# Two query tiles per group of sums over v, chunk-wise decayed keys, and side work dealt in half products

## The chip, the cores and the metric

One NeuronCore of a Trainium2 chip runs the whole kernel as one program. The metric is the device time of one execution in microseconds, from runs of the kernel; lower is better. A profile of one execution gives the engines' instructions: TensorE (PE; its weight loads PEld), VectorE (DVE), ScalarE (ACT), GpSimd (POOL) and SyncE (SP, which issues DMAs here).

## What is computed

A transformer layer on 512 tokens of width 1024, all in float32: a SwiGLU feed-forward (width 2816) with residual and layer norm, a token mixer with residual and layer norm, and a second feed-forward. The mixer adds two gated branches of one input projection:

```python
# sliding window attention, blocks of 128 queries, each against its own and the previous block of keys
scores = einsum('bnqkgd,bnskd->bnkgqs', qb, kb) * 64**-0.5      # masked, with a sink per head
p = exp(scores - m); probs = p / (sum(p) + exp(sink - m))
out = einsum('bnkgqs,bnskd->bnqkgd', probs, vb)                 # 16 query heads, 4 kv heads, width 64
# HGRN2 recurrence, 8 heads of 128, chunks of 64 tokens
f = lb + (1 - lb) * sigmoid(f_logit); k = 1 - f; gc = cumsum(log f)      # within a chunk
q_dec = q * exp(gc); k_inv = k * exp(-gc); k_end = k * exp(g_last - gc)
o = causal(q_dec @ k_inv.T) @ v + q_dec @ state;  state = state * exp(g_last) + k_end.T @ v
y = o * rsqrt(mean(o**2) + eps) * norm_g * silu(og)
merged = sigmoid(gate_a) * (y_attn @ w_pa) + sigmoid(gate_h) * (y @ w_ph);  out = merged @ w_out
```

## The kernel before

Large products keep float32 accuracy with operands split into two rounded halves (`split`, L72): ScalarE casts the high half (`whi`), VectorE subtracts to get the low half (`wlo`), and TensorE runs three matmuls for each pair (`mm3`, L104, and `Quads.mul`, L272). Weights stream through SP's queue as 128 x 1024 slabs (`raw`), five buffers; `whi` and `wlo` have four each. A `quad` (L324) computes a 2 x 2 block product with seven products (Strassen's form), for which VectorE also adds weight blocks (`wsum`, L291). A product is 2 x 12 matmuls of 256 columns. Two of the seven products of a quad are left to the next one (`late`, `flush`). `Pipe` (L233) keeps one product prepared ahead of the one that runs.

Attention and the recurrence are side work. They are written as generators, and `Side` (L201) takes steps of them between products: each `tick` adds `rate` to a credit, and each whole unit buys one step, up to the next `yield`. `drain` takes all that is left. The order in which the program is traced gives each instruction its priority; a planner then orders every engine's queue by these priorities and by when it believes operands to be ready, and each engine works its queue off in that order. `tc.issue_after` fixes one instruction behind another on the same engine.

Attention works in four chunks (two pairs of kv heads, each with two query heads of each half) of four query tiles of 128. For each tile `scores` (L716) makes the scores of four heads in two banks and adds mask and sink; `outputs` (L740) exponentiates, normalises (L757), transposes the weights (`transposed`, L110, matmul line L113), copies them out (L763), and sums over v: for each half of the array's columns (`hf`) and each of one or two key blocks one matmul with 64 stationary columns (L770), all in one bank, then one copy (L773) and a store to `ya_dram`. The next tile's scores are traced before the outputs of this one. `both` mixes in the rope of the next chunk's queries, one step after every fourth.

The recurrence (`heads`, L981) runs per head `decays` (L881) and, one head behind, `recur` (L917). Two tiles of keys, `ei` (inverse decay) and `ke` (decay to the chunk's end), lie one after the other. For each block of 128 tokens, one matmul takes all 128 columns of `ei` (L924) and a second one, with 64 stationary columns of `ke`, replaces the scores between the two chunks of the block (L926). A mask copy, the transposed keys (L936), state updates (L942, L951) and outputs (L957, L959) follow; then ScalarE squares, VectorE reduces, GpSimd raises to the power -1/2 (L968), VectorE scales (L970), TensorE transposes (L973), and y goes to `yh_dram`. Rates are 8, 6, 8 and 12 steps per product. After the last products `sums` projects `ya_dram` (its eight products `run` carry the last side work), then `yh_dram`.

Only these functions change; both feed-forwards share `Quads.mul` but have no side work.

Of the kernel before, what the change touches and what calls it, by code (L numbers as in the profile page):

```python
# [20 lines left out]
P = 128  # L21
# [21 lines left out]
def body(ctx, tc, a):  # L43
# [156 lines left out]

    class Side:  # L201

# [8 lines left out]
        def step(self):  # L211
            while self.queue:
                if next(self.queue[0], self) is not self:
                    return True
                self.queue.pop(0)
            return False

        def tick(self):
            if self.queue:
                self.due += self.rate  # L220
            while self.due >= 1.0:
                self.due -= 1.0
                if not self.step():
                    self.due = 0.0

        def drain(self):
            while self.step():
                pass
            self.due = 0.0
# [3 lines left out]
    class Pipe:  # L233
# [9 lines left out]
        def pump(self, depth=0):  # L243
            while len(self.queue) > depth:
                run, ops = self.queue.pop(0)
                run(ops)
                side.tick()
# [14 lines left out]
    class Quads:  # L262
# [8 lines left out]
        def mul(self, bk, w, n, first, last):  # L271
            wh, wl = (t.rearrange("p (k j c) -> p k j c", j=2, c=P) for t in w)  # L272
            xh, xl = self.x.get(n)
            for j in range(2):
                reg = bk[:, j * 256:(j + 1) * 256]

                def mm(w, x, first=False, last=False):
                    nc.tensor.matmul(reg, lhsT=w, rhs=x, start=first, stop=last, skip_group_check=True)  # L278

                for k in range(4):  # L280
                    mm(wh[:, k, j], xh[:, k], first=first and j == 0 and k == 0)
                    mm(wh[:, k, j], xl[:, k])
                for k in range(4):
                    mm(wl[:, k, j], xh[:, k], last=last and k == 3)

# [311 lines left out]
    def tok_major(src, b_bc, dst):  # L597

        parts = []

        def prep(t):
            if not parts:
                parts.extend(slab(src[i]) for i in range(2))
            return t

        def run(t):
            acc = bank("A")
            for k in range(KT):
                c = (k % 4) * 256
                mm3(acc[:, :256], x1.tok(k, t), [w[:, c:c + 256] for w in parts[k // 4]], k == 0, k == KT - 1)  # L610
            nc.vector.tensor_tensor(out=dst[:, t], in0=acc[:, :256], in1=b_bc, op=ALU.add)
        return lambda t: pipe.push(lambda: prep(t), run)
# [127 lines left out]
    def outputs(pp, n, ip, neg, nm, y):  # L740
# [24 lines left out]
        yield  # L765
        o = bank("B")
        for hf in range(2):
            g = 2 * pp + hf
            for kk in range(kb):
                nc.tensor.matmul(o[hf * HD:(hf + 1) * HD, :256],  # L770
                                 lhsT=v_sb[:, n + 1 - kb + kk, g * HD:(g + 1) * HD],
                                 rhs=pts[kk][:, hf * 256:(hf + 1) * 256], start=kk == 0, stop=kk == kb - 1)
        nc.scalar.copy(out=y, in_=o[:, :256].rearrange("p (i c) -> p i c", i=2))  # L773

    def chunk(pp, ip, qs):
        ahead = yield from scores(pp, 0, ip, qs)
        for n in range(TT):
# [3 lines left out]
            y = room(5, [P, 2, P])  # L781
            yield from outputs(pp, n, ip, *now, y)
            h = 4 * pp + 2 * ip
            nc.sync.dma_start(out=ya_dram[h:h + 2, :, n * P:(n + 1) * P].rearrange("i p c -> p i c"), in_=y)
            yield

    def both(work, other, n):

        res = None
        for i, _ in enumerate(work):  # L790
            yield
# [50 lines left out]
    side.rate = 2.0  # L842
# [16 lines left out]
    def par(t, e):  # L859

        return t.rearrange("p (t e s) -> p t e s", e=2, s=CH)[:, :, e]
# [19 lines left out]
    def decays(h):  # L881
# [15 lines left out]
        func(out=ei, in_=gc, func=AF.Exp, scale=-1.0)  # L897
        nc.vector.tensor_tensor(out=ch(ke), in0=ch(gc)[:, :, CH - 1:CH].broadcast_to([P, NC, CH]), in1=ch(gc),
# [8 lines left out]
        nc.vector.tensor_tensor(out=ei, in0=ei, in1=kk, op=ALU.mult)  # L907
        nc.vector.tensor_tensor(out=ke, in0=ke, in1=kk, op=ALU.mult)
# [6 lines left out]
        return q, ei, ke, q2, de, dd  # L915

    def recur(h, q, ei, ke, q2, de, dd):  # L917
# [3 lines left out]
        sp = bank("B")  # L921
        for t in range(TT):
            tsl = slice(t * P, (t + 1) * P)
# [9 lines left out]
        nc.vector.tensor_tensor(out=par(ke, 0)[:, :TT - 1], in0=par(ke, 0)[:, :TT - 1],  # L933
                                in1=de[1][:, :TT - 1].broadcast_to([P, TT - 1, CH]), op=ALU.mult)
        yield
        kp = transposed([ke[:, t * P:(t + 1) * P] for t in range(TT - 1)])  # L936
# [35 lines left out]
        yield  # L972
# [33 lines left out]
    next_heads(0, 8.0)  # L1006
# [3 lines left out]
    next_heads(1, 6.0)  # L1010
# [6 lines left out]
    next_heads(2, 8.0)  # L1017
    quad_to(a["w_fqg"][5], pairs[3].q, pairs[3].g)
    vals(3)
    next_heads(3, 12.0)  # L1020
# [6 lines left out]
    def sums(n, src, wname, slots, combine):  # L1027
# [165 lines left out]
```

## Time and profile before

| | |
|---|---|
| time, median of 3 runs | 1295.9 us (1295.33 to 1296.37) |
| profiled execution | 1297.03 us, span 1294.9 us |
| PE busy | 1253.3 us, 97% |
| DVE busy | 936.2 us, 72% |
| ACT busy | 626.4 us, 48% |
| attention stage, recurrence stage | 454 to 606 us, 620 to 835 us |

The span runs from the first to the last instruction of the profiled execution. Busy is the union of an engine's instructions; TensorE's matmuls are pipelined, so their records overlap, and a start-to-start distance tells more than a duration. A float32 matmul that is not split leaves two records.

### The profile page before, as it was taken

How to read it: one execution, taken by the hardware profiler on the slowest of the kernel's cores; microseconds unless marked ns; L12 is line 12 of the kernel's file. 1: busy time of each engine (PE TensorE's matmuls, PEld its weight loads, DVE VectorE, ACT ScalarE, POOL GpSimd, SP SyncE). 2: the span in 40 equal slices, each digit the busy share in tenths (PEclk: the TensorE clock that was granted, in tenths of full speed). 3: DMA queues.
4: the chain of work that ended last, by engine and by line, in shares of the span. 5: the costliest groups of instructions: out<-in, count | busy, mean ns of one | idle time of the engine just before them, and what ended most of it. 6: DMA issues, size and time to landing. Idle time of an engine off the chain costs nothing.

```text
span 1294.9 us, 21771 instructions
## 1 busy us (share of the span) xinstructions
PE 1253.3 (97%) x9040; PEld 1170.0 (90%) x9040; DVE 936.2 (72%) x1288; ACT 626.4 (48%) x891; POOL 75.9 (6%) x53
## 2 busy tenths in 40 slices
PE   7999999999998999999999999899999999999997
PEld 7999999988898989898998987788899999998886
DVE  7987878623499998997778776464798787784325
ACT  5645555411156667667653746342355445463110
POOL 2000000000031100100011010000120000000001
PEclk9999999999999999999999999999999999999998
DMA  6424233532233443223223243574233423354211
GB/s 239 134 96 131 83 114 131 179 96 88 94 104 105 144 134 99 91 98 101 71 77 102 83 130 122 168 255 131 98 115 115 128 85 115 102 162 143 84 47 65
DMA packets 53315, 150.75 MB, mean 116 GB/s; under 512 B 5856, under 2 KB 15072, under 8 KB 53216
## 3 DMA queue, kind: packets, MB, share of 16 engines
q1 hardware_dynamic: 49184, 135.72, 32.3%
q10 hardware_dynamic: 4032, 13.63, 3.0%
q8 instruction: 71, 1.16, 0.4%
q14 instruction: 28, 0.23, 0.1%
HBM read 134.65 MB, written 14.68 MB: 115 GB/s over the span
## 4 chain that ended last, share of the span: by engine, by line
PE 56%; DVE 7%; issue 2%; POOL 1%; ACT 1%; DMA 1%; DVEq 0%; SPq 0%; POOLq 0%; ACTq 0%
PE A L278 30%; PE A L106 4%; PE A L108 4%; PE A L107 4%; PE B L107 2%; PE B L106 2%; PE B L108 2%; PE B L113 2%; PE B L770 1%; DVE wlo L75 1%; PE B L924 1%; POOL rs L968 1%; DVE wsum L291 1%; PE B L926 1%; PE B L728 1%
## 5 line engine op out<-in xcount | busy, mean ns | idle before, releaser
L278 PE MATMUL A<-x,whi 128*128 128x256 f32 x3840 | 550.8, 285 | 14.4 <-ACT whi L74 7.5
L278 PEld LDWEIGHTS A<-x,whi 128*128 128x128 f32 x3840 | 499.9, 193 | 20.1 <-ACT whi L74 7.8
L75 DVE TENSOR_TENSOR wlo<-raw,whi 128x1024 fp32r<-128x1024 f32 (+1 forms) x186 | 225.5, 1214 | 185.3 <-ACT whi L74 184.0
L74 ACT CAST whi<-raw 128x1024 fp32r<-128x1024 f32 (+1 forms) x186 | 192.9, 1040 | 324.2 <-PE A L108 132.0
L278 PE MATMUL A<-x,wlo 128*128 128x256 f32 x1920 | 313.3, 284 | 1.6 <-DVE wlo L75 1.6
L278 PEld LDWEIGHTS A<-x,wlo 128*128 128x128 f32 x1920 | 267.2, 193 | 2.5 <-DVE wlo L75 2.0
L74 ACT CAST whi<-wsum 128x1024 fp32r<-128x1024 f32 x128 | 134.3, 1050 | 153.9 <-PE A L278 96.0
L75 DVE TENSOR_TENSOR wlo<-wsum,whi 128x1024 fp32r<-128x1024 f32 x128 | 156.2, 1220 | 12.5 <-ACT whi L74 12.2
L107 PE MATMUL A<-wlo,x 128*128 128x256 f32 (+1 forms) x360 | 115.4, 321 | 0.0
L106 PE MATMUL A<-whi,x 128*128 128x256 f32 (+1 forms) x360 | 115.3, 320 | 0.0
L108 PE MATMUL A<-whi,x 128*128 128x256 f32 (+1 forms) x360 | 115.0, 320 | 0.0
L291 DVE TENSOR_TENSOR wsum<-raw 128x1024 f32<-128x1024 f32 x64 | 87.6, 1373 | 2.7 <-POOL x L129 2.0
L291 DVE TENSOR_TENSOR wsum<-raw,wsum 128x1024 f32<-128x1024 f32 x64 | 78.0, 1218 | 0.8
L106 PEld LDWEIGHTS A<-whi,x 128*128 128x128 f32 x360 | 68.5, 190 | 5.1
L108 PEld LDWEIGHTS A<-whi,x 128*128 128x128 f32 x360 | 68.3, 190 | 4.9
L107 PEld LDWEIGHTS A<-wlo,x 128*128 128x128 f32 x360 | 68.4, 190 | 4.6
L107 PE MATMUL B<-wlo,x 128*128 128x512 f32 (+1 forms) x200 | 69.8, 349 | 0.0
L106 PE MATMUL B<-whi,x 128*128 128x512 f32 (+1 forms) x200 | 69.6, 348 | 0.0
L108 PE MATMUL B<-whi,x 128*128 128x512 f32 (+1 forms) x200 | 69.3, 347 | 0.0
L412 POOL TENSOR_TENSOR rstd<-ve,pw 128x1 f32<-128x1 f32 x12 | 16.2, 1352 | 759.9 <-DVE ve L410 758.6
L106 PE MATMUL A<-x,whi 128*128 128x512 f32 (+1 forms) x160 | 59.8, 374 | 0.0
L107 PE MATMUL A<-x,whi 128*128 128x512 f32 (+1 forms) x160 | 59.3, 371 | 0.0
(172 smaller groups left out, 1536.6 us busy)
## 6 DMA issues: line engine op xcount, KB each, us to landing
raw<-in_w_dram SPq DMA_DIRECT2D x130, 512.0 KB, 3.6
raw<-in_w_fqg_dram SPq DMA_DIRECT2D x24, 512.0 KB, 3.7
raw<-in_w_q_dram SPq DMA_DIRECT2D x8, 512.0 KB, 3.7
raw<-in_w_ga_dram SPq DMA_DIRECT2D x8, 512.0 KB, 3.4
raw<-in_w_gh_dram SPq DMA_DIRECT2D x8, 512.0 KB, 3.8
raw<-in_w_i_dram SPq DMA_DIRECT2D x8, 512.0 KB, 3.8
raw<-in_w_pa_dram SPq DMA_DIRECT2D x8, 512.0 KB, 4.4
g<-x_spill ACTq DMA_DIRECT2D x8, 512.0 KB, 4.5
```

The source lines that it names most:

```text
L74: nc.scalar.copy(out=hi, in_=src)
L75: nc.vector.tensor_tensor(out=lo, in0=src, in1=hi, op=ALU.subtract)
L106: nc.tensor.matmul(out, lhsT=lh, rhs=rh, start=first, stop=False, **kw)
L107: nc.tensor.matmul(out, lhsT=lh, rhs=rl, start=False, stop=False, **kw)
L108: nc.tensor.matmul(out, lhsT=ll, rhs=rh, start=False, stop=last, **kw)
L113: nc.tensor.transpose(out=tp[:, j * P:(j + 1) * P], in_=b, identity=ident)
L278: nc.tensor.matmul(reg, lhsT=w, rhs=x, start=first, stop=last, skip_group_check=True)
L291: nc.vector.tensor_tensor(out=t, in0=x, in1=y, op=ALU.add)
L412: nc.gpsimd.tensor_tensor(out=rstd, in0=ve, in1=pw, op=ALU.pow)
L728: nc.tensor.matmul(out, lhsT=qs[i][:, hf, qsl], rhs=k_hi[pp][:, hf, ksl], start=True, stop=False)
L770: nc.tensor.matmul(o[hf * HD:(hf + 1) * HD, :256], lhsT=v_sb[:, n + 1 - kb + kk, g * HD:(g + 1) * HD], rhs=pts[kk][:, hf * 256:(hf + 1) * ...
L924: nc.tensor.matmul(sp[:, tsl], lhsT=ei[:, tsl], rhs=q[:, tsl], start=True, stop=True)
```

## The change

The side work's credit is now given in shares: half a product's rate in the middle of a product and half at its end, in the projections a quarter after every second of eight key blocks. A step may return `PAUSE`, which ends the tick and leaves the rest of the credit for the next one. Pauses stand behind the normalisation of the attention weights, behind their copies, and behind the normalisation of a head's output. The rates become 3 (attention, was 2), 4, 4, 4 and 9.

`outputs` is cut into `probs` and `weigh`. `weigh` sums over v for two query tiles at once: two banks, one for each half of the columns, 6 or 8 matmuls whose halves alternate, the tile that came last first, all others fixed behind the first. The transposed weights of odd tiles are copied into the rooms of that tile's scores. The output is copied in two halves of 64 partitions, and stored once per two tiles.

In the recurrence `ei` and `ke` lie chunk by chunk in one tile (64 columns of `ei`, 64 of `ke`, and so on). The scores of a block are two matmuls with 128 stationary columns each and 64 moving ones: the first chunk's queries against its `ei` and `ke`, the second chunk's against the first's `ke` and its own `ei`.

```diff
+    PAUSE = object()
         def step(self):
             while self.queue:
-                if next(self.queue[0], self) is not self:
-                    return True
+                r = next(self.queue[0], self)
+                if r is not self:
+                    return r or self
                 self.queue.pop(0)
-            return False
+            return None
-        def tick(self):
+        def tick(self, share):
             if self.queue:
-                self.due += self.rate
+                self.due += self.rate * share
             while self.due >= 1.0:
                 self.due -= 1.0
-                if not self.step():
+                r = self.step()
+                if r is PAUSE:
+                    break
+                if r is None:
                     self.due = 0.0
...
-                run(ops)
-                side.tick()
+                side.tick(run(ops) or 0.5)
...  (Quads.mul)
+                if j == 0:
+                    side.tick(0.5)
...  (tok_major)
+                if k == KT // 2:
+                    side.tick(0.5)
...  (probs, from outputs)
-        yield
+        yield PAUSE
+        tps = [transposed([neg[j // 2][:, j % 2, kk * P:(kk + 1) * P] for j in range(4)]) for kk in range(kb)]
         pts = []
         for kk in range(kb):
-            tp = transposed([neg[j // 2][:, j % 2, kk * P:(kk + 1) * P] for j in range(4)])
-            pt = room(6 + kk)
-            nc.scalar.copy(out=pt, in_=tp)
+            pt = neg[kk].rearrange("p i c -> p (i c)") if n % 2 else room(6 + kk)
+            nc.scalar.copy(out=pt, in_=tps[kk])
             pts.append(pt)
+        return pts
+    def weigh(pp, n, pts, y):
+        o = [bank("B") for _ in range(2)]
+        first = None
+        for i in (1, 0):
+            kb = len(pts[i])
+            for m, kk in enumerate(reversed(range(kb))):
+                for hf in range(2):
+                    g = 2 * pp + hf
+                    with tc.issue_after(first) if first else ExitStack():
+                        mm = nc.tensor.matmul(o[hf][hf * HD:(hf + 1) * HD, i * 256:(i + 1) * 256],
+                                              lhsT=v_sb[:, n + i + 1 - kb + kk, g * HD:(g + 1) * HD],
+                                              rhs=pts[i][kk][:, hf * 256:(hf + 1) * 256], start=m == 0, stop=m == kb - 1)
+                    first = first or mm.ins
         for hf in range(2):
...
+            nc.scalar.copy(out=y[h].rearrange("p i n c -> p n i c"),
+                           in_=o[hf][h].rearrange("p (n i c) -> p n i c", n=2, i=2))
...  (chunk)
+            pts.append((yield from probs(pp, n, ip, *now)))
+            yield PAUSE
+            if n % 2:
+                y = room(5, [P, 2, 2, P])
+                weigh(pp, n - 1, pts[-2:], y)
...  (decays)
-        lf, ke = room(2 + h % 2), room(4 + h % 2)
-        e = big(10 if h % 2 == 0 else 4)
-        eg, ei = e[:, 0], e[:, 1]
+        lf, eg = room(2 + h % 2), room(4 + h % 2)
+        ek = big(10 if h % 2 == 0 else 4, [P, NC, 2, CH])
+        ei, ke = ek[:, :, 0], ek[:, :, 1]
...  (recur)
-            nc.tensor.matmul(sp[:, tsl], lhsT=ei[:, tsl], rhs=q[:, tsl], start=True, stop=True)
-            lo, hi = slice(t * P, t * P + CH), slice(t * P + CH, (t + 1) * P)
-            nc.tensor.matmul(sp[:CH, hi], lhsT=ke[:, lo], rhs=q[:, hi], start=True, stop=True)
+            for e in range(2):
+                c = slice(t * P + e * CH, t * P + (e + 1) * CH)
+                k0 = t * 2 * P + e * CH
+                nc.tensor.matmul(sp[:, c], lhsT=rows[:, k0:k0 + P], rhs=q[:, c], start=True, stop=True)
...  (behind the scaling by rs)
-        yield
+        yield PAUSE
         oT = transposed([on[:, t * P:(t + 1) * P] for t in range(TT)])
...  (sums, run)
+                if k and k % 2 == 0:
+                    side.tick(0.25)
...
+            return 0.25
```

## Rows read from the trace of the kernel before

**Rows 1.** The page's busy table: engine, busy us, share of span, instructions.
```profile
PE 1253.3 (97%) x9040; PEld 1170.0 (90%) x9040; DVE 936.2 (72%) x1288; ACT 626.4 (48%) x891; POOL 75.9 (6%) x53
```

**Rows 2.** Stages: window, length, busy PE, PEld, DVE, ACT, POOL, clock, DMA share, GB/s.
```profile
405.00:454.00 49.00, 45.80 (x379) 45.14 (x378) 48.40 (x77) 32.05 (x53) 5.52 (x3) 1.00 0.42 135
454.00:606.00 152.00, 149.96 (x1165) 135.50 (x1163) 138.56 (x337) 106.01 (x242) 8.59 (x5) 0.99 0.34 104
500.00:525.00 25.00, 25.00 (x209) 23.70 (x208) 19.50 (x44) 18.17 (x39) 0.00 (x0) 1.00 0.38 114
540.00:565.00 25.00, 24.66 (x190) 24.00 (x191) 24.47 (x68) 17.43 (x44) 1.30 (x1) 0.93 0.18 59
620.00:835.00 215.00, 203.80 (x1497) 187.58 (x1496) 154.34 (x230) 115.56 (x156) 18.86 (x16) 1.00 0.32 104
```

**Rows 3.** PE's waits in 405:454 and 620:840: total us, times, longest us.
```profile
PE B L113 <- DVE r L757: 2.2, 1, 2.2
...
PE B L113 <- DVE r L970: 9.4, 7, 2.5
```

**Rows 4.** PE timeline, runs of two and four sums: start, length, operation, count.
```profile
496.77 0.65 PE L770 MATMUL B<-r,g 128*64 128x256 f32 x4
...
507.43 0.64 PE L278 MATMUL A<-x,wlo 128*128 128x256 f32 x4
508.00 1.09 PE L770 MATMUL B<-r,g 128*64 128x256 f32 x8
...
509.24 0.28 PE L729 MATMUL B<-g,g 128*128 128x256 f32 x1
```

**Rows 5.** PE timeline, a cut run and one out of step.
```profile
477.81 0.48 PE L278 MATMUL A<-x,whi 128*128 128x256 f32 x2
478.38 0.65 PE L770 MATMUL B<-r,g 128*64 128x256 f32 x2
478.96 0.38 PE L278 MATMUL A<-x,whi 128*128 128x256 f32 x1
479.27 1.08 PE L770 MATMUL B<-r,g 128*64 128x256 f32 x6
480.29 0.87 PE L113 MATMUL B<-ident,r 128*128 128x128 f32 x6
...
592.15 1.57 PE L770 MATMUL B<-r,g 128*64 128x256 f32 x8
```

**Rows 6.** DVE groups in 454:606: shapes, count, busy us, mean ns.
```profile
L75 DVE TENSOR_TENSOR wlo<-wsum,whi 128x1024 fp32r<-128x1024 f32 x20 | 24.3, 1216 | 0.9 <-ACT whi L74 0.7
...
L75 DVE TENSOR_TENSOR wlo<-raw,whi 128x1024 fp32r<-128x1024 f32 x16 | 19.4, 1215 | 0.7 <-ACT whi L74 0.7
...
L291 DVE TENSOR_TENSOR wsum<-raw,wsum 128x1024 f32<-128x1024 f32 x10 | 12.1, 1214 | 0.0
```

**Rows 7.** One line's instructions: ns min/median/max.
```profile
L773 ACT COPY r<-B x16: 355/373/379, 456.0 to 607.2; 128x256 f32<-128x256 f32 x16
```

**Rows 8.** PE timeline, the scores of one head.
```profile
735.89 0.39 PE L924 MATMUL B<-g,g 128*128 128x128 f32 x2
736.21 0.33 PE L926 MATMUL B<-g,r 128*64 128x64 f32 x2
736.47 0.49 PE L924 MATMUL B<-g,g 128*128 128x128 f32 x2
...
738.50 0.51 PE L278 MATMUL A<-x,whi 128*128 128x256 f32 x2
```

**Rows 9.** PE timeline, a state update.
```profile
808.84 0.83 PE L942 MATMUL B<-g,r 128*128 128x128 f32 x6
809.51 0.61 PE L957 MATMUL B<-g,g 128*128 128x128 f32 x4
```

**Rows 10.** Timelines of SP and ACT where the projections meet.
```profile
833.34 0.32 SPq L977 DMA_DIRECT2D yh_dram<-r  x1
...
839.38 1.05 ACT L74 CAST x<-raw 128x1024 fp32r<-128x1024 f32 x1
844.33 0.57 ACT L1055 COPY g<-A 128x512 f32<-128x512 f32 x1
```

More of the change, by code (lines that the diff above doesn't have):

```diff
@@ L212, in step @@
             while self.queue:
-                if next(self.queue[0], self) is not self:
-                    return True
+                r = next(self.queue[0], self)
+                if r is not self:
+                    return r or self
                 self.queue.pop(0)
-            return False
-        def tick(self):
+            return None
+        def tick(self, share):
             if self.queue:
-                self.due += self.rate
+                self.due += self.rate * share
             while self.due >= 1.0:
                 self.due -= 1.0
-                if not self.step():
+                r = self.step()
+                if r is PAUSE:
+                    break
+                if r is None:
                     self.due = 0.0
         def drain(self):
-            while self.step():
+            while self.step() is not None:
                 pass
@@ L738, in scores, with probs @@
         return neg, nm
-    def outputs(pp, n, ip, neg, nm, y):
+    def probs(pp, n, ip, neg, nm):
         kb = 1 if n == 0 else 2
@@ L757, in outputs @@
             nc.vector.tensor_scalar(out=p_, in0=p_, scalar1=rd[:, j:j + 1], scalar2=None, op0=ALU.mult)
-        yield
+        yield PAUSE
+        tps = [transposed([neg[j // 2][:, j % 2, kk * P:(kk + 1) * P] for j in range(4)]) for kk in range(kb)]
         pts = []
         for kk in range(kb):
-            tp = transposed([neg[j // 2][:, j % 2, kk * P:(kk + 1) * P] for j in range(4)])
-            pt = room(6 + kk)
-            nc.scalar.copy(out=pt, in_=tp)
+            pt = neg[kk].rearrange("p i c -> p (i c)") if n % 2 else room(6 + kk)
+            nc.scalar.copy(out=pt, in_=tps[kk])
             pts.append(pt)
-        yield
-        o = bank("B")
-        for hf in range(2):
[L768 to L773, printed above, removed]
+        return pts
[12 more added lines that the diff above has]
+                    first = first or mm.ins
+        for hf in range(2):
+            h = slice(hf * HD, (hf + 1) * HD)
+            nc.scalar.copy(out=y[h].rearrange("p i n c -> p n i c"),
+                           in_=o[hf][h].rearrange("p (n i c) -> p n i c", n=2, i=2))
     def chunk(pp, ip, qs):
+        h = 4 * pp + 2 * ip
+        pts = []
         ahead = yield from scores(pp, 0, ip, qs)
@@ L780, in chunk @@
                 ahead = yield from scores(pp, n + 1, ip, qs)
[L781 to L785, printed above, removed]
+            pts.append((yield from probs(pp, n, ip, *now)))
[3 more added lines that the diff above has]
+                weigh(pp, n - 1, pts[-2:], y)
+                nc.sync.dma_start(out=ya_dram[h:h + 2, :, (n - 1) * P:(n + 1) * P].rearrange("i p c -> p i c"),
+                                  in_=y.rearrange("p i n c -> p i (n c)"))
+                yield
     def both(work, other, n):
         res = None
-        for i, _ in enumerate(work):
-            yield
+        for i, r in enumerate(work):
+            yield r
             if other and i % n == 0:
@@ L841, in body @@
     side.add(attention())
-    side.rate = 2.0
+    side.rate = 3.0
     gate_quad(1)
@@ L859, in par @@
     def par(t, e):
+        if len(t.shape) == 3:
+            return t.rearrange("p (t e) s -> p t e s", e=2)[:, :, e]
         return t.rearrange("p (t e s) -> p t e s", e=2, s=CH)[:, :, e]
@@ L896, in decays @@
         func(out=eg, in_=gc, func=AF.Exp)
-        func(out=ei, in_=gc, func=AF.Exp, scale=-1.0)
-        nc.vector.tensor_tensor(out=ch(ke), in0=ch(gc)[:, :, CH - 1:CH].broadcast_to([P, NC, CH]), in1=ch(gc),
+        func(out=ei, in_=ch(gc), func=AF.Exp, scale=-1.0)
+        nc.vector.tensor_tensor(out=ke, in0=ch(gc)[:, :, CH - 1:CH].broadcast_to([P, NC, CH]), in1=ch(gc),
                                 op=ALU.subtract)
@@ L906, in decays @@
         nc.vector.tensor_tensor(out=q, in0=q, in1=eg, op=ALU.mult)
-        nc.vector.tensor_tensor(out=ei, in0=ei, in1=kk, op=ALU.mult)
-        nc.vector.tensor_tensor(out=ke, in0=ke, in1=kk, op=ALU.mult)
+        nc.vector.tensor_tensor(out=ei, in0=ei, in1=ch(kk), op=ALU.mult)
+        nc.vector.tensor_tensor(out=ke, in0=ke, in1=ch(kk), op=ALU.mult)
         yield
@@ L914, in decays, with recur @@
         yield
-        return q, ei, ke, q2, de, dd
-    def recur(h, q, ei, ke, q2, de, dd):
+        return q, ek, q2, de, dd
+    def recur(h, q, ek, q2, de, dd):
         p = pairs[h // 2]
@@ L921, in recur @@
         sp = bank("B")
+        rows = ek.rearrange("p c a s -> p (c a s)")
         for t in range(TT):
-            tsl = slice(t * P, (t + 1) * P)
-            nc.tensor.matmul(sp[:, tsl], lhsT=ei[:, tsl], rhs=q[:, tsl], start=True, stop=True)
-            lo, hi = slice(t * P, t * P + CH), slice(t * P + CH, (t + 1) * P)
-            nc.tensor.matmul(sp[:CH, hi], lhsT=ke[:, lo], rhs=q[:, hi], start=True, stop=True)
+            for e in range(2):
+                c = slice(t * P + e * CH, t * P + (e + 1) * CH)
+                k0 = t * 2 * P + e * CH
+                nc.tensor.matmul(sp[:, c], lhsT=rows[:, k0:k0 + P], rhs=q[:, c], start=True, stop=True)
         yield
@@ L931, in recur @@
                                   data=sp.rearrange("p (t c) -> p t c", c=P))
-        nc.vector.tensor_tensor(out=par(ke, 0)[:, :TT - 1], in0=par(ke, 0)[:, :TT - 1],
+        nc.vector.tensor_tensor(out=par(ek[:, :, 0], 1)[:, :TT - 1], in0=par(ek[:, :, 1], 0)[:, :TT - 1],
                                 in1=de[1][:, :TT - 1].broadcast_to([P, TT - 1, CH]), op=ALU.mult)
         yield
-        kp = transposed([ke[:, t * P:(t + 1) * P] for t in range(TT - 1)])
+        kp = transposed([rows[:, (2 * t + 1) * P:(2 * t + 2) * P] for t in range(TT - 1)])
         keT = room(6)
@@ L971, in recur @@
                                 in1=rs.rearrange("p (t o) -> p t o", o=1).broadcast_to([P, TT, P]), op=ALU.mult)
-        yield
+        yield PAUSE
         oT = transposed([on[:, t * P:(t + 1) * P] for t in range(TT)])
@@ L1005, in body @@
     vals(0)
-    next_heads(0, 8.0)
+    next_heads(0, 4.0)
     quad_to(a["w_fqg"][2], pairs[1].q, pairs[1].g)
@@ L1009, in body @@
     pairs[2] = Pair(0)
-    next_heads(1, 6.0)
+    next_heads(1, 4.0)
     quad_to(a["w_fqg"][3], pairs[2].f, pairs[2].q)
@@ L1016, in body @@
     quad_to(a["w_fqg"][4], pairs[2].g, pairs[3].f)
-    next_heads(2, 8.0)
+    next_heads(2, 4.0)
     quad_to(a["w_fqg"][5], pairs[3].q, pairs[3].g)
     vals(3)
-    next_heads(3, 12.0)
+    next_heads(3, 9.0)
     side.add(last_head())
```

## Prediction

> **What bounds the kernel now.** I read the page's busy table first, then busy time by stage, then TensorE's waits, then TensorE's own timeline at the places that the diff touches. The busy table says that TensorE is occupied for 97% of the span [rows 1], so a change pays only if it takes work or waits off TensorE, and only where no other engine is equally full. By stage the picture splits. In the attention stage (454 to 606 us) TensorE is occupied for 149.96 of 152 us and VectorE for 138.56, 91%; in single stretches VectorE is at 98% (540 to 565) or 78% (500 to 525), and before the stage at 99% [rows 2]. In the recurrence stage (620 to 835 us) TensorE is occupied for 203.8 of 215 us and VectorE only for 154.3, 72% [rows 2]: there a saving on TensorE is a saving of time. Of the 11.2 us that TensorE idles in that stage, 9.4 us at seven places are the transposes of the normalised outputs (L113) waiting for L970 [rows 3], which itself waits for GpSimd's power (L968).
>
> Busy is not the same as useful: the timeline shows what TensorE pays for matmuls that fill half of its columns, the sums over v (L770) and the cross-chunk scores (L926). Each of their matmuls leaves two records (passes).
>
> **Part 1: sums over v of two query tiles as one group.** Today each of the 16 tile steps (4 chunks of 4 query tiles) has its own run. A run of four matmuls in good order: four L278 start from 507.43 on, 0.12 apart, so the next would be due at 507.91; the second full-width matmul behind the run starts at 509.24, 0.12 after the first should; the run costs 509.24 - 0.12 - 507.91 = 1.21 us [rows 4]. A run of two (first tile, one key block) is 0.65 long against 1.09 [rows 4], so a matmul costs (1.09 - 0.65)/2 = 0.22, and going into and out of half-width work 1.21 - 4 x 0.22 = 0.33. That is 0.11 a pass of 256 columns, half of what the passes cost one by one in a run out of step (1.57 long [rows 5]): the two head halves run side by side today already, where their order allows it. Where the copy of the second key block arrives late, the planner cuts the run in two, one L278 between: from 478.13 (two L278 start at 477.81, the second here 0.2 later, as the first behind a transpose) to 480.29 less 0.12 and plus the way out, some 2.1 us [rows 5]; six are cut, read the same way 2.1 to 2.33, together 13.6. Two more are out of step, 1.7 each. With four runs of two (0.77) and four good ones (1.2) that is 3.1 + 4.8 + 3.4 + 13.6 = 24.9 us.
>
> After: per chunk one group of 6 matmuls and one of 8, the halves always in alternation, since all stand behind the first and the first waits for the last copy. 14 x 0.22 + 2 x 0.33 = 3.74, times 4 chunks 14.9 us. TensorE needs 10.0 us less.
>
> How much of it becomes time is VectorE's question. A product costs VectorE one wlo (1.216) and 4/7 of a wsum (1.21) [rows 6], with its output adds about 2.0 us; 36 of them stand in the stage (20 and 16 wlo), which leaves 138.6 - 72 = 66.6 us for 15 tile steps, 4.4 each, rope included. At the old rate of 2 side steps a product, a tile step (5 of its own, 1.5 of rope) has 3.25 products beside it: VectorE 10.9; TensorE 3.25 x 24 x 0.12 = 9.4, scores 0.96, transposes 0.87, sums 1.55, together 12.7. At rate 3 and 4.5 + 1.5 steps it has two: VectorE 8.4; TensorE 5.8 + 0.96 + 0.87 + 0.93 = 8.5. So the stage turns from bound by TensorE into a tie. At VectorE's best share (98%) a step takes 8.6 and 16 steps lose 1 us of the 10; at 91% it takes 9.2, and 12 us go. Bounds of this part: -2 to 10 us. I take 95%, between the two shares and what a stage that waits for VectorE should reach: 8.84, 5 us lost, 5 us gained.
>
> Hidden edits: the two output copies of a group are 64 x 512 instead of 128 x 256 (0.373 each, 16 of them [rows 7]); at twice the time each ScalarE gets 6 us more on 106 of 152 [rows 2]. The ya stores fall from 16 to 8 of twice the size, so SP's queue gets shorter, and nobody reads ya before the projections. The odd tile's weights stay in the rooms of its scores until the group has read them, so the scores two tiles on wait for it; two products per tile step cover that.
>
> **Part 2: decayed keys chunk by chunk.** Per head four full-width matmuls (L924) and four half-width ones (L926) alternate, 735.89 to 738.50, 2.61 us [rows 8]. After: eight full-width matmuls of 64 moving columns, 16 passes. The nearest row is the state update, six passes of 128 moving columns in 809.51 - 808.84 = 0.67, 0.112 a pass [rows 9]. Upper bound 0.112: 1.79 us, saved 0.82 a head. Lower bound half of it, if the pace follows the moving columns: saved 1.71. I take 0.112, because these passes have the same 128 stationary columns as that row: 8 x 0.82 = 6.6 us, up to 13.7. With VectorE at 72% it is all time. The VectorE and ScalarE instructions keep number and size; their operands come in runs of 64 elements, which I cost at nothing (at worst some 4 us on VectorE, which has 60 to spare [rows 2]).
>
> [...]
>
> **Part 3: half products and pauses.** The pause behind the normalisation puts half a product (12 x 0.12 = 1.44 us), in the projection a quarter (6 matmuls, 1.3 us), between L970 and its transposes. Of seven waits with 9.4 us, the longest 2.5 [rows 3], only what exceeds that is left, 1 to 1.5 us: saved 8. Bounds: 0, if the planner draws the transposes forward all the same, to 9.4. The pauses in attention face one wait, 2.2 us of L113 on L757 before 454 [rows 3], where VectorE is at 99% and TensorE would wait for it anyway: 0.
>
> The lower rates (4 for 8 and 6; 9 for 12) have a price only if side work misses its stage. A stage has 36 steps and 9 to 11 products of 4: it just fits. In the last one, 46 steps at 2.25 a quarter end in the sixth of eight products, not after the fourth. Today the last head is stored at 833.34 and read back and cast from 839.38 on, the last product is copied out at 844.33 [rows 10], and these rows of y are needed first three quarters into the next product, 3.9 us later: some 6 us are to spare. I cost it at 0, at worst 5.
>
> **Sum.** 5 + 6.6 + 8 = 19.6 us. The profiled execution took 1297.03 us (span 1294.9), so 1277.4 on its basis; on that of the median, 1295.9, it is 1276.
>
> **Rivals.** (a) VectorE doesn't hold attention back: 10 + 6.6 + 9.4, 1270. For: 13 us of idle time on VectorE in 454 to 606. Against: a tie leaves nothing over. (b) The pauses, or attention, give nothing: without the pauses 1295.9 - 5 - 6.6 = 1284, without attention 1281. For: the planner decides the order on each engine, and what it believes ready may go early again. (c) The score passes go by their moving columns, at half the pace of rows 9: 5 + 13.7 + 8, 1269. [...] (d) Slower: in attention VectorE's queue is held up by its own waits as in 500 to 525, 78 to 80%, while it is the bound. A tile step then takes 8.4/0.80 = 10.5 us in place of 8.5; 16 x 2.0 = 32 us of waiting for wlo stand against the 24.6 that the parts take off TensorE: 1303. It decides from a share below 84%. Against it: that stretch had TensorE full, so VectorE's idle time there cost nothing and says little.
>
> **Chances.** Forecast (1271 to 1283) 0.50, (a) 0.17, (b) to 1289 0.16, (c) 0.05, (d) 0.07, no change 0.05. The range, 1264 to 1287, leaves out (d), no change and the far end of (b). A measurement of this kernel tells 0.2% (2.6 us) from no change: faster 0.88, same 0.05, slower 0.07.
>
> **What would show it.** Right: L770 in eight groups of 12 or 16 records, none cut; no other half-width records; a head's scores in about 1.8 us; waits of L113 on L970 under 2 us in sum; 620 to 835 shorter by 14 us or so, attention by about 5. Wrong: new waits of L278 on wlo above 10 us in attention (part 1), L113 on L970 still near 9 us (part 3), a wait of the second projection on its y (rates), score passes well under 0.1 us (part 2).

## The result

The changed kernel took 1280.97 us against 1296.13 us of the kernel before on the same chip: ratio 0.9876 (0.9863 to 0.9888; the quotient of these two medians alone is 0.9883), 15.2 us or 1.2% faster. The forecast was 1276, its range 1264 to 1287. The profiled executions took 1297.03 before and 1279.68 after.

The page's busy table after [rows 1], then busy time by stage (columns as in [rows 2]); the stages are shorter, so the windows are too:

```profile
PE 1239.9 (97%) x9040; PEld 1167.8 (91%) x9040; DVE 934.7 (73%) x1288; ACT 628.3 (49%) x891; POOL 74.1 (6%) x53
```

```profile
404.00:452.00 48.00, 45.62 (x376) 44.88 (x375) 47.44 (x87) 33.42 (x62) 6.35 (x3) 1.00 0.34 110
452.00:597.00 145.00, 141.48 (x1148) 132.03 (x1147) 135.33 (x325) 106.32 (x232) 8.23 (x6) 0.99 0.36 114
611.00:820.00 209.00, 200.76 (x1524) 190.20 (x1524) 156.58 (x232) 118.49 (x158) 16.70 (x16) 1.00 0.34 109
```

TensorE still has 9040 instructions, with 13.4 us less in them. The waits of TensorE in 404 to 611 and in 597 to 880 (total, times, longest; us) answer to [rows 3]. L1005 is L970 of before, L769 is L757, L738 the scores of attention, L721 the rope of the queries:

```profile
PE B L738 <- DVE g L721: 3.0, 3, 2.2
PE B L113 <- DVE r L769: 2.6, 4, 1.4
...
PE B L113 <- DVE r L1005: 7.7, 8, 1.5
PE B L113 <- DVE g L968: 0.4, 1, 0.4
```

The 9.4 us of L113 behind the normalisation became 7.7; most of them stayed. TensorE's timeline shows one group of sums (L790), which answers to [rows 4, 5], and one head's scores (L961), which answer to [rows 8]:

```profile
501.40 0.64 PE L284 MATMUL A<-x,wlo 128*128 128x256 f32 x4
501.96 1.95 PE L790 MATMUL B<-r,g 128*64 128x256 f32 x16
503.84 1.22 PE L284 MATMUL A<-x,whi 128*128 128x256 f32 x8
...
728.19 0.64 PE L284 MATMUL A<-x,wlo 128*128 128x256 f32 x4
728.67 1.90 PE L961 MATMUL B<-g,g 128*128 128x64 f32 x16
730.37 0.84 PE L284 MATMUL A<-x,whi 128*128 128x256 f32 x5
```

The sums now come in eight groups of 12 or 16 records, none cut. Read as the prediction read them, they cost 1.65 and 2.07 us, 14.9 in all, as forecast. A head's scores take 1.70 us from their start to that of the next large matmul (728.67 to 730.37), in all eight heads within 0.01; the same reading of a head that runs without a break gave 2.61 before. That is 0.106 us for each of 16 passes (forecast 0.112) and 8 x 0.91 = 7.3 us in all.

Where the time went: I cut the traces at the same large matmuls (L278 and L106 to L108 before, counted in the order in which TensorE ran them: the 2850th, 4050th and 5500th), so each stretch holds the same large work. The first stretch begins with the first of them and the last ends with the start of the last. Every row is one profiled execution; the first stretch has the same instructions in all kernels and still scatters between 402.0 and 404.7 us, so a us or two in one of the next columns can be scatter.

| stretch, us | to 2850 | attention, 2850 to 4050 | recurrence, 4050 to 5500 | rest |
|---|---|---|---|---|
| before | 403.1 | 202.1 | 274.7 | 400.2 |
| after | 402.0 | 196.5 | 264.4 | 400.3 |

Attention gave 5.6 us and the recurrence with the first projection 10.3. The last 400 us are the same.

### The profile page after: what moved, and what is told of

Its sections match the earlier page's. It is cut to its first block, busy times and chain, and to the rows that moved or that the text cites. A ratio compares the mean times of both kernels' runs of the same rounds, so it can differ in the third digit from the quotient of the medians.

```text
span 1277.8 us, 21726 instructions
## 1 busy us (share of the span) xinstructions
PE 1239.9 (97%) x9040; PEld 1167.8 (91%) x9040; DVE 934.7 (73%) x1288; ACT 628.3 (49%) x891; POOL 74.1 (6%) x53
## 4 chain that ended last, share of the span: by engine, by line
PE 52%; DVE 11%; issue 2%; ACT 2%; POOL 1%; DVEq 0%; POOLq 0%; ACTq 0%
PE A L284 27%; PE A L106 4%; PE A L107 4%; PE A L108 4%; DVE wlo L75 2%; PE B L107 2%; PE B L106 2%; PE B L108 2%; PE B L113 2%; DVE wsum L299 2%; PE B L961 1%; PE B L790 1%; POOL rs L1003 1%; DVE g L721 1%; DVE r L743 1%
## 5 line engine op out<-in xcount | busy, mean ns | idle before, releaser
L106 PE MATMUL A<-whi,x 128*128 128x256 f32 (+1 forms) x360 | 115.7, 321 | 0.0
L108 PE MATMUL A<-whi,x 128*128 128x256 f32 (+1 forms) x360 | 114.9, 320 | 0.0
L106 PEld LDWEIGHTS A<-whi,x 128*128 128x128 f32 x360 | 68.5, 190 | 5.0
L108 PEld LDWEIGHTS A<-whi,x 128*128 128x128 f32 x360 | 68.3, 190 | 4.9
L106 PE MATMUL B<-whi,x 128*128 128x512 f32 (+1 forms) x200 | 69.7, 348 | 0.0
L108 PE MATMUL B<-whi,x 128*128 128x512 f32 (+1 forms) x200 | 69.4, 347 | 0.0
L106 PE MATMUL A<-x,whi 128*128 128x512 f32 (+1 forms) x160 | 59.5, 372 | 0.0
L108 PE MATMUL A<-x,wlo 128*128 128x512 f32 (+1 forms) x160 | 59.3, 371 | 0.0
```

The source lines that it names most:

```text
L106: nc.tensor.matmul(out, lhsT=lh, rhs=rh, start=first, stop=False, **kw)
L108: nc.tensor.matmul(out, lhsT=ll, rhs=rh, start=False, stop=last, **kw)
```

## Experiments

All ratios are to the kernel before on the same chip, with 95% intervals; each comes from five rounds, the two light kernels' from three. The expectations speak of a before of 1296 us; where it took longer, compare the differences.

**One part at a time.** Theory: the three terms of the forecast are right and add up. Rivals: the groups alone give nothing, and what part 3 gives comes from half products and rates and not from the pauses.

`e1_scores_only` is the kernel before with part 2:

```diff
-        e = big(10 if h % 2 == 0 else 4)
-        eg, ei = e[:, 0], e[:, 1]
+        ek = big(10 if h % 2 == 0 else 4, [P, NC, 2, CH])
+        ei, ke = ek[:, :, 0], ek[:, :, 1]
...
-            nc.tensor.matmul(sp[:, tsl], lhsT=ei[:, tsl], rhs=q[:, tsl], start=True, stop=True)
...
-            nc.tensor.matmul(sp[:CH, hi], lhsT=ke[:, lo], rhs=q[:, hi], start=True, stop=True)
...
+                nc.tensor.matmul(sp[:, c], lhsT=rows[:, k0:k0 + P], rhs=q[:, c], start=True, stop=True)
```

> The kernel before with the chunk-wise decayed keys alone (part 2). Theory: a head's scores fall from 2.6 to 1.8 us on TensorE, all of it becomes time: 6.6 us less than before, about 1289.5. The waits of the transposes on L970's counterpart stay near 9 us. Rival (the saving is hidden, because VectorE or the chain of a head sets the recurrence stage): under 3 us, 1293 or more.

Measured: 1290.66 against 1298.37, ratio 0.9937 (0.9918 to 0.9956), 7.7 us. Its recurrence took 267.2 us, 7.5 less than before, attention 202.4. Forecast 6.6: right, and the waits of L113 stayed at 9.1.

`e2_group_only` is the kernel before with `probs` and `weigh` (part 1), whole products and rate 2:

```diff
-            yield from outputs(pp, n, ip, *now, y)
...
+            pts.append((yield from probs(pp, n, ip, *now)))
...
+            if n % 2:
+                y = room(5, [P, 2, 2, P])
+                weigh(pp, n - 1, pts[-2:], y)
```

> The kernel before with the grouped sums over v alone (part 1), side work dealt as before. Theory: TensorE needs 10 us less, of which VectorE lets 5 to 6 become time: 1290 to 1291. Rival (VectorE does not hold attention back): 10 us less, 1286. Rival (the gain in attention comes from the new dealing, not from the groups): no change, 1296.

Measured: 1297.63 against 1298.37, ratio 0.9991 (0.998 to 1.0002). The theory fell: in the time the groups alone are worth 0.7 us, by the interval at most 2.6. TensorE's timeline in this kernel shows a place where the gain goes, the first scores of the second pair of query heads, which wait for their rope (L711):

```profile
535.06 0.40 PE L278 MATMUL A<-x,whi 128*128 128x256 f32 x2
539.10 0.48 PE L728 MATMUL B<-g,g 128*128 128x128 f32 x1 [3.65 <-DVE g L711]
```

TensorE stands still for 3.65 us (longest such wait before 1.4). I counted start to start in the attention stretch and took off the pace of the work itself (0.12 us a large matmul or score, 0.109 a transpose, 0.108 a pass of sums). What is left fell by 8 us around the sums, as it does after; it rose by 4.1 at these scores and by 2 to 3 at other steps, so that 1.2 us stayed. Of the 4.1, 2.3 are the longer wait; most of the rest is that TensorE's clock had fallen there (see the granted clock below). After, the longest wait of this kind is 2.2.

`e3_deal_only` is the kernel before with half products, pauses and the new rates:

```diff
-    side.rate = 2.0
+    side.rate = 3.0
...
+                if j == 0:
+                    side.tick(0.5)
...
-        yield
+        yield PAUSE
```

> The kernel before with the new dealing alone (half products, pauses, rates), sums and scores as before. Theory: the planner places the transposes by when it believes them ready, so pauses move next to nothing: 1294 to 1297, waits of the transposes on L970's counterpart 7 to 10 us in sum. Rival (the pauses took the 1.7 us of waits and more that the changed kernel has less): 1290 to 1293. Rival (the dealing costs time that the other parts pay back): 1299 or more.

Measured: 1292.56 against 1298.37, ratio 0.9955 (0.9937 to 0.9973), 5.8 us. That is the rival's figure. Waits of TensorE in 605 to 880:

```profile
PE B L113 <- DVE r L980: 7.0, 7, 1.5
```

`e4_old_deal` is the changed kernel with whole products, no pauses and the old rates:

```diff
-                if j == 0:
-                    side.tick(0.5)
...
-    side.rate = 3.0
+    side.rate = 2.0
```

> The changed kernel with the side work dealt as before (whole products, no pauses, rates 2, 8, 6, 8, 12); groups and chunk-wise keys kept. Theory: parts 1 and 2 make the whole gain: 1281 to 1284. Rival (dealing matters): 1287 or more.

Measured: 1288.68 against 1298.37, ratio 0.992 (0.9901 to 0.9939), 9.7 us below before; from 1296 that is 1286.3, between the two and next to the rival. So the dealing is worth 0.45% alone and 0.992 less 0.9876, 0.44%, on top of parts 1 and 2: 5.7 us either way. What in it does this, half products or the lower rates of the recurrence, no run separates; the pauses are next. The groups are worth 0.09% alone and 0.17% on top of part 2. By the times the three parts add up, 0.63 + 0.09 + 0.45 = 1.17% of the 1.24%; each has its 0.1 to 0.2% of uncertainty.

**Pauses and rates.** Theory: the planner places an instruction by when it believes its operands to be ready, so a pause doesn't move it; the rate matters more. The rival keeps the pauses as the cause.

`e5_no_pause` is the changed kernel with plain steps in place of the three pauses:

```diff
-        yield PAUSE
+        yield
```

> The changed kernel with its three pauses as plain steps; half products and rates kept. Theory: pauses are nothing, since the planner places an instruction by when it believes it ready: within 1.5 us of the changed kernel (1280 to 1283 where before is 1296), waits of the transposes of a head's output 7 to 8.5 us in sum as there. Rival (pauses make a part of the gain of the dealing, about 5 us): 1285 to 1288.

Measured: 1282.06 against 1297.10, ratio 0.9887 (0.9871 to 0.9904); the changed kernel has 0.9876. On TensorE the number of large matmuls between a head's last output and its transposes is the same in all eight heads with and without pauses, 35, 37, 21, 33, 23, 15, 20 and 13 (before: 38, 39, 22, 33, 25, 15, 19, 15). In the recurrence a single pause moves nothing: there TensorE's whole order is the same, and L113 waits for L1005 for 7.9 us. In attention the pauses do change the order, between 451 and 596 us; the stretch took 198.0 us against 196.5, and the times can't tell the two kernels apart.

`e6_rate2` and `e10_rate4` are the changed kernel with another rate in attention:

```diff
-    side.rate = 3.0
+    side.rate = 2.0
```

> The changed kernel with 2 side steps per product in attention instead of 3. Theory of the prediction (rate 3 turns the stage into a tie with VectorE, so a lower rate would not be worse): 1278 to 1282 where before is 1296. Rival, after the runs of the single parts (groups give 1.2 us alone, dealing 1.3 us, both 5.6 us in this stage: only the higher rate lets the groups' saving through, since otherwise side work is left over at the stage's end and behind the second block of queries): 1284 to 1287.

```diff
-    side.rate = 3.0
+    side.rate = 4.0
```

> The changed kernel with 4 side steps per product in attention instead of 3. Theory (rate 3 already ends the first two chunks before the second block of queries is there, and this block sets the second half): within 1.5 us of the changed kernel, 1280 to 1283 where before is 1296. Rival (a higher rate keeps paying, as from 2 to 3): 1276 to 1279. Rival (VectorE's tie): 1285 or more.

Measured: rate 2 took 1287.40 against 1297.10, 0.9919 (0.9902 to 0.9936), and rate 4 took 1288.58 against 1297.71, 0.993 (0.9917 to 0.9942). Both are about half a per cent slower than rate 3, so my theories (no difference at rate 4, nothing worse at rate 2) fell. Attention took 199.3 and 201.5 us in them, 196.5 at rate 3. At rate 4 scores and transposes come earlier and wait more; TensorE's waits in 405 to 611 at rate 4:

```profile
PE B L113 <- DVE r L769: 3.7, 3, 2.5
PE B L738 <- DVE g L721: 3.6, 3, 2.2
PE A L284 <- ACT whi L74: 3.3, 1, 3.3
```

The first two were 2.6 and 3.0 after; the third is a product that stands for want of its weights. At rate 2 the same window has 3.6 us in one wait for L721 and 3.3 us of products that wait for L304 and `wlo`:

```profile
PE B L738 <- DVE g L721: 3.6, 1, 3.6
PE A L284 <- ACT vs L304: 2.0, 1, 2.0
PE A L284 <- DVE wlo L75: 1.3, 1, 1.3
```

At rate 4 the waits of this window are 11.1 us in sum, after 5.6, which is about the 5 us by which the stretch is longer; at rate 2 they are only 2 to 3 us more than after, and the clock has to be read with them. No run isolates either.

**TensorE's granted clock.** Up to its last large matmul TensorE ran at 2.4 GHz but for single stretches of 3.41 or 6.83 us at 1.2 GHz, in which large matmuls start 0.21 us apart in place of 0.12 (e2, 755.37 to 756.65). The prediction's rows had one, the 0.93 of 540 to 565 [rows 2]. Windows, first one of before and then three of e2 (the third figure from the end is the clock as a share of 2.4 GHz):

```profile
540.80:544.10 3.30, 3.30 (x15) 3.30 (x16) 3.30 (x11) 2.45 (x9) 0.00 (x0) 0.50 0.02 5
```

```profile
453.30:456.60 3.30, 3.30 (x16) 3.30 (x17) 2.25 (x9) 1.21 (x4) 0.00 (x0) 0.50 0.54 175
538.60:545.30 6.70, 6.20 (x28) 6.20 (x29) 5.56 (x20) 4.10 (x12) 0.00 (x0) 0.50 0.04 14
750.20:756.90 6.70, 6.70 (x30) 6.02 (x30) 5.52 (x10) 3.59 (x5) 0.70 (x1) 0.50 0.27 97
```

In e2 the clock fell at 453.20, as a wait of 2.20 us for L759 ended, at 538.54, within the wait of 3.65 us shown above, and at 750.16, 1.7 us after a wait of 1.43 us. Before has the same wait of 2.2 us [rows 3] without a fall, so the wait alone doesn't decide it. Time at 1.2 GHz in each stretch of the table above; at most half of it is lost:

| stretch, us (of it at 1.2 GHz) | attention | recurrence |
|---|---|---|
| before | 202.1 (3.4) | 274.7 (0) |
| after | 196.5 (3.4) | 264.4 (0) |
| e2, groups alone | 200.9 (10.2) | 276.8 (6.8) |
| e3, dealing alone | 200.8 (3.4) | 272.4 (0) |
| e4, groups and scores | 200.8 (10.2) | 268.7 (3.4) |
| e6, rate 2 | 199.3 (6.8) | 266.2 (3.4) |
| e10, rate 4 | 201.5 (0) | 266.3 (3.4) |

So e2 lost up to 3.4 us more than before in either stretch, in the recurrence with unchanged code. Without that the groups alone give some 4.6 us in attention. The runs agree: at a mean granted clock of 0.990 or 0.991 the six runs of e2 have a median of 1297.2 us, the five of before on that chip 1300.9. Time plotted against the mean clock, one slope for all kernels of a chip and one level for each, puts e1 7.2, e2 3.7, e3 3.5 and e4 11.0 us below before at equal clock, e5 (rate 3) 13.7 and e6 (rate 2) 13.0, each to about 1 us. This is an estimate, as no run held the clock. By it the groups and the scores add up to e4, and rate 2 is hardly worse than rate 3 but for the clock.

**Is VectorE the bound of attention?** The prediction said so: it took 5 of 10 us away for it. Theory of these two runs: TensorE and its waits for late operands decide, and VectorE can be lightened without effect.

`e7_light_before` and `e8_light_after` leave out the division of the attention weights:

```diff
-        for j in range(4):
-            p_ = neg[j // 2][:, j % 2, :kb * P]
-            nc.vector.tensor_scalar(out=p_, in0=p_, scalar1=rd[:, j:j + 1], scalar2=None, op0=ALU.mult)
```

> The kernel before without the division of the attention weights (64 VectorE instructions, 17 us of its time; the weights stay unnormalised). If VectorE bounds attention: 5 us or more below before, at most 1291. If TensorE and waits bound it: 1293 to 1297, about the 2.2 us that TensorE waited for these instructions.

> The changed kernel without the division of the attention weights (as in the kernel before without it). If VectorE holds back half of the groups' saving: 5 us or more below the changed kernel, 1276 or less where before is 1296, and the attention stage 9 to 10 us shorter than in the kernel before without the division. If waits on the chain of rope and softmax hold it back: within 3 us of the changed kernel, and the stage about 5.6 us shorter than there.

Measured: 1297.24 and 1280.34 against 1297.10, ratios 0.9999 (0.9988 to 1.001) and 0.9869 (0.9849 to 0.9888); the kernels that they start from have 1 and 0.9876. The stage's windows of the lighter kernels, first the one from before, then the one from after:

```profile
454.00:606.00 152.00, 149.97 (x1167) 136.36 (x1166) 120.55 (x274) 107.96 (x245) 9.48 (x6) 0.99 0.33 103
```

```profile
452.00:600.00 148.00, 143.77 (x1175) 135.32 (x1174) 124.20 (x270) 110.53 (x239) 10.36 (x6) 0.99 0.35 112
```

VectorE was relieved of 18 us in 152 [rows 2] and TensorE had the same 149.97 us to do: no gain. In the changed kernel it was relieved of some 14 us (135.33 in 145 is 138 in 148), which moved the time by less than its interval. The attention stretch took 200.5 and 194.9 us, 1.6 less than in either parent, within the scatter, and 5.6 apart as before and after are: what was expected if late operands hold the stage back. VectorE, at 93%, holds nothing back on average.

**The wait that stayed.** L113 waits for L1005, and that for a chain over ScalarE, VectorE and GpSimd. All engines of the changed kernel, one head:

```profile
738.75 0.69 DVE L999 TENSOR_REDUCE ss<-r 128x4 f32<-128x512 f32 x1 [0.22 <-ACT r L997]
...
740.48 0.15 DVE L1001 TENSOR_SCALAR ss<-ss 128x4 f32<-128x4 f32 x1
...
740.77 1.84 POOL L1003 TENSOR_TENSOR rs<-ss,pw 128x4 f32<-128x4 f32 x1 [10.21 <-DVE ss L1001]
742.65 0.69 DVE L1005 TENSOR_TENSOR r<-B,rs 128x512 f32<-128x512 f32 x1 [0.90 <-POOL rs L1003]
743.39 0.66 PE L113 MATMUL B<-ident,r 128*128 128x128 f32 x4 [1.42 <-DVE r L1005]
```

The chain runs for 4.6 us from L999 on; large matmuls cover most of it and 1.42 us are left, the size of half a product (1.44 us). A pause that put half a product in between would have covered nearly all of these waits, of which the longest is 1.5; it put nothing there. To push the transposes back for real takes many pauses, so that the credit of several halves passes in between.

`e9_seven_pauses`: seven pauses in place of one behind the scaling by rs, with rates that still finish the work:

```diff
         yield PAUSE
+        yield PAUSE   # six such lines
         oT = transposed([on[:, t * P:(t + 1) * P] for t in range(TT)])
...
-    next_heads(0, 4.0)   # likewise 1 and 2
+    next_heads(0, 8.0)   # likewise 1 and 2
...
-    next_heads(3, 9.0)
+    next_heads(3, 16.0)
```

> The changed kernel with seven pauses instead of one ahead of the transposes of a head's output, and rates of 8, 8, 8 and 16 in the recurrence to pay for them. One pause does not change the planned order at these places at all; seven put 28 to 56 large matmuls between a head's last output matmul and its transposes, where the changed kernel has 13 to 37. Theory (the waits on L970's counterpart are the planner's too early placing): they fall from 7.7 to under 2.5 us, time 4 to 6 us below the changed kernel, 1275 to 1278 where before is 1296. Rival (the waits are TensorE's spare time and turn up elsewhere): within 1.5 us of the changed kernel.

Measured: 1279.62 against 1297.71, 0.9861 (0.9846 to 0.9876), not the 4 to 6 us below the changed kernel; the two intervals overlap. TensorE's waits in 605 to 880:

```profile
PE A L106 <- ACT whi L74: 3.0, 2, 2.4
PE B L113 <- DVE g L968: 0.9, 2, 0.7
PE B L961 <- DVE g L940: 0.8, 1, 0.8
PE B L113 <- DVE r L1005: 0.5, 1, 0.5
```

The planned distance grew to 45, 46, 32, 56, 51, 28, 30 and 36 large matmuls and the wait fell from 7.7 us to 0.5. But it comes back at another place, the second projection. SP, ACT and PE of this kernel there (time, length, what it waited for):

```profile
814.43 0.32 SPq L1018 DMA_DIRECT2D yh_dram<-r  x1
817.13 0.37 SPq L1072 DMA_DIRECT2D raw<-yh_dram  x1
821.21 1.04 ACT L74 CAST x<-raw 128x1024 fp32r<-128x1024 f32 x1 [4.71 <-DMA raw<-yh_dram]
823.74 0.50 PE L106 MATMUL A<-x,whi 128*128 128x512 f32 x1 [2.42 <-ACT whi L74]
```

The last head's transposes stand 36 large matmuls ahead of the one that waits here, in the changed kernel 57, and the projection which reads them stands 2.4 us. At 825.31, 1.6 us after this wait, the clock fell to 1.2 GHz for 3.41 us, which costs up to 1.7 more. What the prediction named as the price of late side work is real.

`e12_dosed_pauses` keeps the pauses but gives the last heads fewer, and a higher last rate:

```diff
-        yield PAUSE
+        for _ in range((6, 9, 4)[h - 5] if h > 4 else 7):
+            yield PAUSE
...
-    next_heads(3, 9.0)
+    next_heads(3, 20.0)   # the others 8.0
```

> The changed kernel with seven pauses ahead of the transposes of heads 0 to 4 and 6, 9 and 4 for heads 5, 6 and 7, rates 8, 8, 8 and 20. The last transposes stand behind large matmul 5262 in the planned order (5259 in the changed kernel, 5280 with seven pauses for every head). Theory (seven pauses took 7.2 us of waits away and gave 3.5 us back, since the last head's y came too late for the second projection): waits on L970's counterpart under 2 us, no wait of the second projection, 1275 to 1278 where before is 1296, 4 to 6 us below the changed kernel. Rival (recurrence waits are made up by others wherever they go): within 2 us of the changed kernel.

Measured: 1275.94 against 1297.76, 0.9835 (0.9822 to 0.9849), 0.4% or some 5 us below the changed kernel, and the best of all versions. The waits in 605 to 880:

```profile
PE B L113 <- DVE r L1005: 1.8, 2, 1.3
PE B L961 <- DVE g L940: 0.8, 1, 0.8
PE A L108 <- DVE wlo L75: 0.5, 1, 0.5
```

The recurrence took 259.5 us, 4.9 less than after, with none of it at 1.2 GHz in either. So most of the 9.4 us of waits were there to be had; the change as it stands didn't take them. The pauses came with higher rates, and these alone were not run; e4, with rates of 8, 6, 8 and 12 and no pauses, has 37, 38, 23, 33, 23, 15, 16 and 11 large matmuls at these places and 9.1 us of waits, so a higher rate by itself doesn't seem to make the distance.

`e11_pool_two` is the changed kernel with the step ahead of the power on GpSimd too, so that the chain leaves VectorE one step earlier:

```diff
-        nc.vector.tensor_scalar(out=ss, in0=ss, scalar1=1.0 / P, scalar2=RMS_EPS, op0=ALU.mult, op1=ALU.add)
+        nc.gpsimd.tensor_scalar(out=ss, in0=ss, scalar1=1.0 / P, scalar2=RMS_EPS, op0=ALU.mult, op1=ALU.add)
```

> The changed kernel with the scaling ahead of GpSimd's power moved from VectorE to GpSimd, so that the chain from a head's outputs to its transposes does not stand behind a weight's subtraction on VectorE (1.0 us in five of eight heads). Theory (the planner draws the transposes forward as soon as it believes the chain shorter): waits of 6 us or more remain, time within 2 us of the changed kernel. Rival (a shorter chain is a shorter wait): waits under 4 us, 1276 to 1278 where before is 1296.

Measured: 1281.77 against 1297.71, 0.9879 (0.9865 to 0.9892), no gain, L113's waits (whole span) rose:

```profile
PE B L113 <- DVE r L1005: 9.3, 8, 1.7
```

The planned distance shrank with the chain that the planner believed in (31, 33, 21, 23, 23, 12, 19, 13): it draws the transposes forward, and they wait a little longer.

## Why the prediction was right, and where its steps were not

The total was right within 5 us of 20: forecast 19.6, measured 15.2 (17.4 between the profiled executions). That is in part luck: one of the three terms was right, one had its size for another reason than the one given, and for the third something else stood in. The time alone doesn't even tell the forecast from rival (b) without a gain in attention, 1281.

**Part 2 was right, mechanism and size.** 6.6 us forecast, 7.3 by the timeline, 7.7 in e1 (by its two times). The passes of 64 moving columns kept about the pace of the row chosen, 0.106 us against 0.112. Rival (c), half that pace, fell. The Trainium skill ("TensorE: Matmul & The Clock Gate", section "Back-to-back issue gap") says that in a stream of weight loads and matmuls the spacing is set by both, and not by the moving columns alone. The trace agrees as far as it goes: half the moving columns with the same 128 stationary ones brought 0.106 us in place of 0.112.

**Part 1: the sums were right, the step behind them was not.** Fewer sums saved what was forecast on TensorE (24.9 to 14.9, 8.1 of the 10 visible around the sums themselves). The step that failed is "How much of it becomes time is VectorE's question". It reckoned a tie with VectorE at 95%. e7 and e8 show that VectorE is not the limit. What stopped half of the gain is late operands of single steps, the second block's rope above all (3.65 us in e2, 1.4 before); and at such waits the granted clock fell, which the prediction didn't price at all. In the time the groups alone gave 0.7 us, not 5; at equal clock they gave an estimated 3.7, in attention's profile 4.6. With the dealing's 1.3 there (200.8 in e3 against 202.1) that is about attention's 5.6 us, so the two add up, and what the dealing does for the groups beyond that is mainly to spare them the fall of the clock. This is worked out from profiles and not isolated: a kernel with parts 2 and 3 but without the groups was not run. Rival (a), which had VectorE out of the way and expected all 10, was right that VectorE isn't the limit and wrong about the time.

**Part 3: the mechanism was wrong, and a neighbour of it gave most of the size.** The step "the pause behind the normalisation puts half a product between L970 and its transposes" failed. It put nothing between them (e5: same order), for rival (b)'s reason: the planner places by when it believes operands to be ready, and a step traced one pause later is not held back by that. e11, where a shorter chain drew the transposes forward, fits this. 9.4 us of waiting went to 7.7, not under 2. In place of 8 us by pauses there were 5.7 by the dealing (e3; e4 against after), and the profiles put them into both stages: 1.3 us in attention and 2.3 in the recurrence by e3, 4.3 and 4.3 by e4, of which up to 3.4 and 1.7 are the clock; 0.9 and 2.6 stay. So an estimated 3.5 us come from the order and some 2 from a clock that fell less often. In attention rate 3 beats 2 and 4 by some 6 us of the time, rate 2 for the larger part through the clock. The prediction had priced half products and rates by themselves at 0.

**Hidden edits held.** A copy of a group takes 0.58 us for the same data on half as many partitions, 64 x 512 in place of 128 x 256 (0.373 [rows 7]), less than the doubling that was feared, and the last head was stored in time in the changed kernel: no wait of TensorE at the second projection, only 0.9 us of ScalarE. e9 shows how near that edge is.

**Rival (d)**, slower by VectorE's queue, did not come: the waits of 404 to 611 above hold no product that waits for `wlo`.

## What to carry to other kernels

A pause in the order of a program moves an instruction only where its planner lets it; read the planned distance between producer and consumer (how many matmuls lie between) before and after, and price the edit by that. A busy share of 91 to 95% on a second engine doesn't make it the bound: lighten it by a tenth and see whether the time moves. Before a part is called worthless, compare the granted clock of its runs with that of the others: a saving can be there and be eaten by a clock that fell at a wait. When a wait is pushed away, find what reads the pushed result next, and leave it the slack (e9 against e12).

## What the runs showed of the hardware

Score passes with 64 moving columns cost nearly as much as with 128: 0.106 us each against 0.112 ([rows 9] and the scores above), with 128 stationary columns in both; the range that the prediction left open downwards, to half of it, is closed here. GpSimd's power on 128 x 4 elements took 1.0 to 1.9 us, 1.84 in the chain above: the longest instruction in the chain that L113 waits for there (spans on GpSimd are rough). TensorE's granted clock fell to 1.2 GHz for 3.41 or 6.83 us at a time; in e2 each of the three falls between 450 and 760 us came during a wait of 1.4 to 3.7 us or within 1.8 us of its end, and such a wait doesn't always bring one.
